# A decoder trunk's feed-forward: its second product by seven products of halves instead of eight

## The chip, the cores and the metric

The kernel runs on one core of a Trainium2 chip. Five engines work side by side, each through its own instructions in order: TensorE (PE, matrix products into PSUM banks), VectorE (DVE, elementwise work), ScalarE (ACT, activation functions and copies), GpSimd (POOL) and SyncE (SP, which here only issues transfers). They wait for each other by semaphores. Transfers between the main memory (HBM) and the on-chip memory (SBUF) are issued by SP, ACT or POOL and carried out by 16 DMA engines. The metric is the device time of one execution in microseconds.

## The reference

A trunk of two layers over 512 tokens of width 1024, in float32. Each layer first mixes the tokens (a gated linear recurrence beside one kind of attention in the first layer, a gated convolutional recurrence beside another kind in the second), projects, adds, normalises; then comes the feed-forward that matters here:

```python
def swiglu(x, w13, w2):
    a, b = jnp.split(x @ w13, 2, axis=-1)
    return (jax.nn.silu(a) * b) @ w2
...
x = layer_norm(ALPHA * x + swiglu(x, ffn_w13[layer], ffn_w2[layer]), ln_g[layer, 1], ln_b[layer, 1])
```

The inner width is 2816, 22 blocks of 128. The first product (gate and up) makes the inner activations, the second (`w2`, 2816 x 1024) brings them back to width 1024. ALPHA is the square root of 2.

## The kernel before, in words

**Three matmuls for one.** PE works in a fast rounded float32 form. To keep the accuracy every operand is split into a rounded high half and a low half (the rest); `mm3` (L252) multiplies high by high, high by low and low by high. A weight tile of 128 x 1024 is loaded by SP into a staging tile `ws` (two of them), ACT copies the high half into `wh`, DVE subtracts for the low half `wl` (`weights`, L231; five buffers each of `wh` and `wl`). A buffer comes free when PE has done the matmuls that read it, and ACT and DVE work in order, so a split that waits for its buffer or its transfer holds up what is queued behind it. Activations are split in the same way by `put` (L247).

**The feed-forward** (`ffn`, L393) takes the 22 inner blocks in parts. For each block of a part, gate and up are made with the inner block on the partitions and the 512 tokens along the free axis: 8 blocks of the width, `mm3` each, into two banks named `pf` (pair `g` for even blocks, pair `s` for odd). ACT applies the SiLU, DVE multiplies by the other bank, `put` splits the result into `hh` and `hl`. When a part's blocks are done, `out_stream` (L375) does its share of the second product: for each half of the 1024 output columns four banks, one for each 128 tokens, gather over the part's blocks, activations held in PE, 512 weight columns moving. Then `add_res` (L327) adds the four banks to the residual `xt` on DVE. The part that comes last goes through `out_rows` (L335), which finishes one token block after the other, since the normalisation follows it. The parts are 6, 6, 6 and 4 blocks in layer 0 and 4, 6, 6 and 6 in layer 1 (`W2_PARTS`, L52).

**The order** of the work on each engine is set by a scheduler that follows the program with priorities; weight splits get a slightly higher one. SP's loads run ahead as far as staging tiles are free. POOL has little to do: constants at the start, some small transfers of 4 KB in the first layer, and one small power (`rs`) for each token block of a normalisation.

## Time and profile before

| | us |
|---|---|
| median of 3 runs | 1257.22 (1256.35 to 1257.58) |
| the profiled execution | 1257.87 |
| its span, first to last instruction | 1256.1 |

| stretch of the span (us) | PE busy | DVE busy | ACT busy | DMA share |
|---|---|---|---|---|
| 297 to 660, feed-forward of layer 0 | 362.81 of 363.00 | 149.35 | 96.63 | 0.32 |
| 890 to 1240, feed-forward of layer 1 | 350.00 of 350.00 | 139.06 | 89.37 | 0.30 |

The granted clock of PE is 0.995 of full speed over the span, and 1.00 in both stretches. Busy means that at least one instruction was at work on the engine. PE's matmuls overlap, so the length of one in the profile is not the time by which it delays the next. "A <- B" in a wait names who waited and who ended the wait. An idle engine that nobody waits for costs nothing.

### The profile page before, as it was taken

To read this page: it belongs to the slowest core of one execution; us is meant where nothing else is said; L and a number is where in the kernel's file an instruction comes from. 1 tells how busy PE (TensorE), PEld (TensorE's weight loads), DVE (VectorE), ACT (ScalarE), POOL (GpSimd) and SP (SyncE) were. 2 spreads that over 40 slices of the span, in tenths; PEclk is the share of its full clock that TensorE was granted. 3 is DMA by queue.
4 is the path that set the end of the run, shared out by engine and by line. 5 is a ranking of instruction groups with operands and counts; after the bars stand their busy time and mean duration, and the time that the engine had idled before them with its cause. 6 is when DMAs were issued, how large, how long until landed. Compare 5 with 4: busy or idle time off the path is not lost.

```text
span 1256.1 us, 15372 instructions
## 1 busy us (share of the span) xinstructions
PE 1233.1 (98%) x6215; PEld 1003.6 (80%) x6215; DVE 689.3 (55%) x1037; ACT 483.2 (38%) x738; POOL 27.1 (2%) x49
## 2 busy tenths in 40 slices
PE   8999999999999999999999998999999999999997
PEld 6787777679888888888888776778988888888886
DVE  6638789668233324334388596687734333324346
ACT  6446567533222222222233757672322222222220
POOL 2000000000000000000000000000000000000001
PEclk9999999999999999999999998999999999999999
DMA  6421211234233233323324231102423333333221
GB/s 239 151 71 56 77 52 51 78 91 151 67 101 89 96 101 101 95 91 101 101 87 131 68 100 34 51 17 84 152 69 100 101 100 90 96 101 101 94 74 67
DMA packets 35271, 115.45 MB, mean 92 GB/s; under 512 B 4208, under 2 KB 5616, under 8 KB 35200
## 3 DMA queue, kind: packets, MB, share of 16 engines
q1 hardware_dynamic: 33648, 112.70, 28.7%
q10 hardware_dynamic: 1296, 1.73, 0.4%
q8 instruction: 49, 0.80, 0.3%
q14 instruction: 22, 0.18, 0.0%
q0 software_dynamic: 256, 0.03, 0.0%
HBM read 112.32 MB, written 2.10 MB: 91 GB/s over the span
## 4 chain that ended last, share of the span: by engine, by line
PE 89%; DVE 6%; ACT 2%; DMA 2%; issue 1%; SPq 0%; DVEq 0%; ACTq 0%
PE pf L255 13%; PE pf L254 13%; PE pf L256 13%; PE po L256 8%; PE po L254 8%; PE po L255 8%; PE pj L255 4%; PE pj L254 4%; PE pj L256 4%; DMA ws<-in_wst 1%; PE sc L528 1%; PE pv L255 1%; PE pv L254 1%; PE pv L256 1%; PE tr L321 1%; PE cu L840 1%
## 5 line engine op out<-in xcount | busy, mean ns | idle before, releaser
L243 ACT CAST wh<-ws 128x1024 fp32r<-128x1024 f32 x175 | 183.9, 1051 | 517.5 <-PE pf L255 182.9
L244 DVE TENSOR_TENSOR wl<-ws,wh 128x1024 fp32r<-128x1024 f32 x175 | 214.2, 1224 | 289.8 <-ACT wh L243 283.8
L255 PE MATMUL pf<-xl,wh 128*128 128x512 f32 x640 | 249.3, 390 | 0.0
L254 PE MATMUL pf<-xh,wh 128*128 128x512 f32 x640 | 249.3, 390 | 0.0
L256 PE MATMUL pf<-xh,wl 128*128 128x512 f32 x640 | 249.3, 390 | 0.0
L256 PEld LDWEIGHTS pf<-xh,wl 128*128 128x128 f32 x640 | 120.2, 188 | 24.9
L255 PEld LDWEIGHTS pf<-xl,wh 128*128 128x128 f32 x640 | 120.2, 188 | 24.9
L254 PEld LDWEIGHTS pf<-xh,wh 128*128 128x128 f32 x640 | 120.2, 188 | 24.7
L254 PE MATMUL po<-wh,hh 128*128 128x512 f32 x336 | 131.2, 390 | 0.0
L256 PE MATMUL po<-wh,hl 128*128 128x512 f32 x336 | 130.9, 390 | 0.2 <-DVE hl L250 0.2
L255 PE MATMUL po<-wl,hh 128*128 128x512 f32 x336 | 130.9, 390 | 0.0
L422 DVE TENSOR_TENSOR s<-s,pf 128x512 f32<-128x512 f32 x44 | 30.3, 688 | 147.3 <-PE pf L256 147.3
L254 PE MATMUL pj<-xh,wh 128*128 128x512 f32 x256 | 104.2, 407 | 2.8 <-DVE qk L617 1.2
L255 PE MATMUL pj<-xl,wh 128*128 128x512 f32 x256 | 103.6, 405 | 0.2 <-DVE xl L250 0.2
L256 PE MATMUL pj<-xh,wl 128*128 128x512 f32 x256 | 103.8, 405 | 0.0
L256 PEld LDWEIGHTS po<-wh,hl 128*128 128x128 f32 x336 | 63.0, 188 | 13.6 <-DVE hl L250 0.6
L254 PEld LDWEIGHTS po<-wh,hh 128*128 128x128 f32 x336 | 63.1, 188 | 13.1 <-ACT hh L249 0.2
L255 PEld LDWEIGHTS po<-wl,hh 128*128 128x128 f32 x336 | 63.1, 188 | 12.9
L254 PEld LDWEIGHTS pj<-xh,wh 128*128 128x128 f32 x256 | 48.5, 189 | 14.3 <-issue 3.0
L256 PEld LDWEIGHTS pj<-xh,wl 128*128 128x128 f32 x256 | 48.4, 189 | 10.1 <-issue 1.6
L255 PEld LDWEIGHTS pj<-xl,wh 128*128 128x128 f32 x256 | 48.4, 189 | 10.0 <-issue 1.1
L332 DVE TENSOR_TENSOR xt<-xt,po 128x512 f32<-128x512 f32 x64 | 43.3, 684 | 22.8 <-PE po L256 22.8
(245 smaller groups left out, 1830.1 us busy)
## 6 DMA issues: line engine op xcount, KB each, us to landing
ws<-in_wst SPq DMA_DIRECT2D x189, 512.0 KB, 3.5
gb<-in_lnp SPq DMA_DIRECT2D x8, 512.0 KB, 5.0
ws<-in_wst SPq DMA_DIRECT2D x11, 256.0 KB, 5.2
xt<-in_xT SPq DMA_DIRECT2D x8, 256.0 KB, 5.6
xt<-in_x SPq DMA_DIRECT2D x1, 2048.0 KB, 8.1
out_y<-xt SPq DMA_DIRECT2D x4, 256.0 KB, 2.0
out_y<-xt ACTq DMA_DIRECT2D x4, 256.0 KB, 2.0
gw<-in_gw ACTq DMA_DIRECT2D x2, 256.0 KB, 2.7
```

The costliest lines, as they stand in the source:

```text
L243: nc.scalar.copy(hi, st)
L244: nc.vector.tensor_tensor(lo, st, hi.bitcast(F32), ALU.subtract)
L254: mm(ps, ah, bh, start=first, stop=False)
L255: mm(ps, ah, bl, start=False, stop=False)
L256: mm(ps, al, bh, start=False, stop=last)
L321: nc.tensor.transpose(ps[:, j * P:(j + 1) * P], y[:, h * T + j * P:h * T + (j + 1) * P], self.ident)
L332: self.nc.vector.tensor_tensor(y, y, ps, ALU.add)
L422: nc.vector.tensor_tensor(s, s, pb, ALU.mult)
L528: nc.tensor.matmul(ps[u:u + 64, g * 256 + c * 64:g * 256 + (c + 1) * 64], E[:, c * P + u:c * P + u + 64], rhs, start=True, stop=True)
L840: nc.tensor.matmul(ps[:, c:c + m], w, x[:, oi:oi + m], start=n == 0 and x is sh, stop=n == len(mms) - 1 and x is sl)
```

## The change

The second product of two parts of 8 inner blocks in each layer is done by a scheme of seven products of halves. The parts become 8, 8, 2 and 4 blocks in layer 0 and 8, 8 and 6 in layer 1. Only the parts of 8 use the new scheme; the others go on as before.

The inner blocks of such a part form four pairs of an even and an odd block. Write u for the even block's activations and v for the odd one's, 0 and 1 for the first and second 256 tokens, and W11, W12, W21, W22 for the weights (first digit: even or odd block, second: first or second half of the output columns). Instead of the eight products of a half with a half there are seven, of these activations ("forms") with these sums:

| product | activations | weights | bank pair | goes to (token half, column half) |
|---|---|---|---|---|
| 1 | u0 | W11 | a | + (1,1), and stays in a |
| 2 | v1-u1 | W11+W12 | c | - (2,2), and stays in c |
| 3 | s2 = u1-u0-v1 | W11+W12+W22 | a, on top | - (1,2) |
| 4 | s4 = u0-u1+v1-v0 | W22 | c, on top | - (1,2) |
| 5 | u0-u1 | W22+W12 | a, on top | - (2,2) |
| 6 | v0 | W21 | d | + (1,1) |
| 7 | v1 | W11+W12+W22+W21 | a, on top | + (2,1) |

The bank pairs hold two blocks of 128 tokens each; a is `sc` and `ho`, c is `pt` and `po`, d the two banks of `s`. What stays in a bank is added to by the next product that uses it, after DVE has read the bank into `xt`.

The weight sums are made by transfers. Two held tiles (x, one for each two pairs of blocks) begin as W11; when ACT and DVE have split a held tile, POOL issues a transfer that adds the next weights from HBM into it, and it is split again. Two more (y) begin as W22 and get W12 added. The tiles take the places `wah` and `wal`, the split halves go through `wh` and `wl` as before. `forms` makes the differences on DVE when a pair of blocks is done and splits each into halves.

```diff
@@ -49,7 +49,9 @@
 BANKS = {"g": 2, "s": 2, "sc": 1, "ho": 1, "pt": 1, "po": 1}
 EARLY = (S_IA, S_IA + 1, S_IA + 2, S_IA + 3)
 
-W2_PARTS = (((0, 6), (6, 12), (12, 18), (18, 22)), ((0, 4), (4, 10), (10, 16), (16, 22)))
+W2_PARTS = (((0, 8), (8, 16), (16, 18), (18, 22)), ((0, 8), (8, 16), (16, 22)))
+H2 = T // 2
 
 
 class Trunk:
@@ -249,11 +251,11 @@
         self.nc.scalar.copy(hi, dst)
         self.nc.vector.tensor_tensor(lo, dst, hi.bitcast(F32), ALU.subtract)
 
-    def mm3(self, ps, ah, al, bh, bl, first, last):
+    def mm3(self, ps, ah, al, bh, bl, first, last, **kw):
         mm = self.nc.tensor.matmul
-        mm(ps, ah, bh, start=first, stop=False)
-        mm(ps, ah, bl, start=False, stop=False)
-        mm(ps, al, bh, start=False, stop=last)
+        mm(ps, ah, bh, start=first, stop=False, **kw)
+        mm(ps, ah, bl, start=False, stop=False, **kw)
+        mm(ps, al, bh, start=False, stop=last, **kw)
 
     def gemm_ws(self, w, ps, c0=0, c1=T):
         hi, lo = w
@@ -324,12 +326,12 @@
             nc.scalar.copy(self.xh[o], pv)
             nc.vector.tensor_tensor(self.xl[o], pv, self.xh[o].bitcast(F32), ALU.subtract)
 
-    def add_res(self, tb, h, ps, first):
+    def add_res(self, tb, h, ps, first, op=ALU.add):
         y = self.xt[:, tb, h * T:(h + 1) * T]
         if first:
-            self.nc.vector.scalar_tensor_tensor(y, y, ALPHA, ps, ALU.mult, ALU.add)
+            self.nc.vector.scalar_tensor_tensor(y, y, ALPHA, ps, ALU.mult, op)
         else:
-            self.nc.vector.tensor_tensor(y, y, ps, ALU.add)
+            self.nc.vector.tensor_tensor(y, y, ps, op)
 
 
     def out_rows(self, acts, base, lnidx=None, nxt=None, fin=False):
@@ -390,12 +392,119 @@
                 self.add_res(tb, h, pss[tb], first)
 
 
+    def fm(self, tag):
+        if tag == "act":
+            return self.sb.tile([P, 2, H2], F32R, tag="act", bufs=16, name=self.nm("fm"))
+        return self.t2k("fm", [P, 2, H2], F32R, "fm")
+    def put2(self, src):
+        hi, lo = self.fm("act"), self.fm("fm")
+        self.put(src, hi, lo)
+        return hi, lo
+    def forms(self, s):
+        nc = self.nc
+        q = s.rearrange("p a (h t) -> p (a h) t", t=H2)
+        uv = self.put2(q[:, 0:4:2, :])
+        d = self.t2k("d", [P, 2, H2], tag="d")
+        nc.vector.tensor_tensor(d, q[:, 0:4:3, :], q[:, 1:2, :].to_broadcast([P, 2, H2]), ALU.subtract)
+        dd = self.put2(d)
+        v1 = self.fm("act")
+        self.put(q[:, 3, :], v1[:, 0, :], v1[:, 1, :])
+        nc.vector.scalar_tensor_tensor(q[:, 1, :], d[:, 0, :], -1.0, q[:, 3, :], ALU.mult, ALU.subtract)
+        nc.vector.scalar_tensor_tensor(q[:, 0, :], q[:, 1, :], -1.0, q[:, 2, :], ALU.mult, ALU.subtract)
+        ee = self.put2(q[:, 0:2, :])
+        at = lambda p, i: (p[0][:, i, :], p[1][:, i, :])
+        return {"u0": at(uv, 0), "v0": at(uv, 1), "u0-u1": at(dd, 0), "v1-u1": at(dd, 1),
+                "s4": at(ee, 0), "s2": at(ee, 1), "v1": (v1[:, 0, :], v1[:, 1, :])}
+    def products7(self, fs, base, first):
+        nc = self.nc
+        n = len(fs)
+        seen = set()
+        def load(dst, j, k, c, add=False):
+            m = base + (k - 1) * n + 2 * c
+            src = self.ins["wst"][m:m + 2, :, (j - 1) * T:j * T].rearrange("m p t -> p m t")
+            dst = dst.rearrange("p (m t) -> p m t", t=T)
+            if add:
+                nc.gpsimd.dma_start(dst, src, accum_op=ALU.add)
+            else:
+                nc.sync.dma_start(dst, src)
+        def split(st):
+            hi, lo = [self.sb.tile([P, D], F32R, tag=t, bufs=5, name=self.nm(t)) for t in ("wh", "wl")]
+            with self.tc.high_priority(offset=self.hp):
+                self.put(st, hi, lo)
+            return hi, lo
+        def held(tag, j):
+            ts = [self.t2k("w" + tag, [P, D], tag=tag) for _ in range(n // 2)]
+            for c, t in enumerate(ts):
+                load(t, j, j, c)
+            return ts
+        def plain(j, k):
+            ws = []
+            for c in range(n // 2):
+                st = self.sb.tile([P, D], F32, tag="ws", bufs=2, name=self.nm("ws"))
+                load(st, j, k, c)
+                ws.append(split(st))
+            return ws
+        def summed(ts, nxt=None):
+            ws = []
+            for c, t in enumerate(ts):
+                ws.append(split(t))
+                if nxt:
+                    load(t, *nxt, c, True)
+            return ws
+        def product(ws, name, ps, start=False, stop=False):
+            for m, f in enumerate(fs):
+                (hi, lo), (ah, al) = ws[m // 2], f[name]
+                c = slice(m % 2 * T, m % 2 * T + T)
+                for b in range(2):
+                    t = slice(b * P, (b + 1) * P)
+                    self.mm3(ps[b], ah[:, t], al[:, t], hi[:, c], lo[:, c], start and m == 0, stop and m == n - 1,
+                             skip_group_check=True)
+        def result(i, k, ps, op):
+            for b in range(2):
+                self.add_res(2 * (i - 1) + b, k - 1, ps[b], first and (i, k) not in seen, op)
+            seen.add((i, k))
+        a = [self.bank(t, "fa") for t in ("sc", "ho")]
+        c = [self.bank(t, "fc") for t in ("pt", "po")]
+        x, y = held("wah", 1), held("wal", 2)
+        product(summed(x, (1, 2)), "u0", a, True)
+        result(1, 1, a, ALU.add)
+        product(summed(x, (2, 2)), "v1-u1", c, True)
+        result(2, 2, c, ALU.subtract)
+        product(summed(x, (2, 1)), "s2", a)
+        result(1, 2, a, ALU.subtract)
+        product(summed(y, (1, 2)), "s4", c, stop=True)
+        result(1, 2, c, ALU.subtract)
+        product(summed(y), "u0-u1", a)
+        result(2, 2, a, ALU.subtract)
+        d = [self.bank("s", "fd") for _ in range(2)]
+        product(plain(2, 1), "v0", d, True, True)
+        result(1, 1, d, ALU.add)
+        product(summed(x), "v1", a, stop=True)
+        result(2, 1, a, ALU.add)
     def ffn(self, base, wa, lnidx, nxt=None):
         nc = self.nc
         idx = base
         parts = W2_PARTS[nxt is None]
         for pi, (k0, k1) in enumerate(parts):
-            acts = []
+            seven = k1 - k0 == 8
+            acts, fs = [], []
             blocks = list(range(k0, k1))
             if pi == 0:
                 groups = [[0, 1]] + [[k] for k in range(2, k1)]
@@ -415,17 +524,23 @@
                 else:
                     for w, ps in zip(ws, pss):
                         self.gemm_ws(w, ps)
-                for i in range(len(g)):
+                for i, k in enumerate(g):
                     pa, pb = pss[2 * i], pss[2 * i + 1]
-                    s = self.t2k("s", tag="s")
-                    nc.scalar.activation(s, pa, AF.Silu)
-                    nc.vector.tensor_tensor(s, s, pb, ALU.mult)
-                    hh, hl = self.act("hh"), self.act("hl")
-                    self.put(s, hh, hl)
-                    acts.append((hh, hl))
-            last = pi == len(parts) - 1
-            if last:
+                    if k % 2 == 0:
+                        s = self.t2k("s", [P, 2, T], tag="s")
+                    h = s[:, k % 2, :]
+                    nc.scalar.activation(h, pa, AF.Silu)
+                    nc.vector.tensor_tensor(h, h, pb, ALU.mult)
+                    if not seven:
+                        hh, hl = self.act("hh"), self.act("hl")
+                        self.put(h, hh, hl)
+                        acts.append((hh, hl))
+                    elif k % 2:
+                        fs.append(self.forms(s))
+            if pi == len(parts) - 1:
                 wa = self.out_rows(acts, idx, lnidx, nxt, nxt is None)
+            elif seven:
+                self.products7(fs, idx, pi == 0)
             else:
                 self.out_stream(acts, idx, pi == 0)
             idx += k1 - k0
@@ -881,13 +996,13 @@
     with t.phase("l0", v=8, p=2, pT=1, E=5, bb=1, kq=1, G=1, acc=1, ks=1, es=1) as t.ph, \
             tc.tile_pool(name="odd", bufs=1) as t.odd:
         y = t.layer0()
-    with t.phase("f0", s=3, wah=4, wal=4) as t.ph:
+    with t.phase("f0", s=2, d=1, fm=12, wah=4, wal=4) as t.ph:
         wa = t.out_rows(y, S_WO0 + 4, 0, S_FFN0)
         wa = t.ffn(S_FFN0, wa, 1, S_XR)
         xr = t.proj_halves(wa)
     with t.phase("l1", v=4, qk=7, kz=2, z=6, l=4, sh=5, sl=5) as t.ph:
         y = t.layer1(xr)
-    with t.phase("f1", s=3, wah=4, wal=4) as t.ph:
+    with t.phase("f1", s=2, d=1, fm=12, wah=4, wal=4) as t.ph:
         wa = t.out_rows(y, S_WO1 + 4, 2, S_FFN1)
         t.ffn(S_FFN1, wa, 3)
```

Three places show how the instructions move. First POOL: in layer 0, behind the powers of the first normalisation (`rs`). Before, the next powers follow at once:

```order
L310 TENSOR_TENSOR rs_2690<-ve_2688,nhalf 128x1 [waits DVE_49,Activation_49]
L310 TENSOR_TENSOR rs_2745<-ve_2743,nhalf 128x1 [waits DVE_49,Activation_49]
L310 TENSOR_TENSOR rs_5017<-ve_5015,nhalf 128x1 [waits DVE_49,Pool_49]
L310 TENSOR_TENSOR rs_5072<-ve_5070,nhalf 128x1 [waits DVE_49,Pool_49]
L310 TENSOR_TENSOR rs_5139<-ve_5137,nhalf 128x1 [waits DVE_49,Pool_49]
```

After the change there are the adding transfers (`wwah` are the held tiles x, `wwal` the tiles y; the eight of the first part, and the first of the second):

```order
L312 TENSOR_TENSOR rs_2745<-ve_2743,nhalf 128x1 [waits DVE_49,Activation_49]
L436 DMA wwah_3433<-in_wst 128x2x512 [waits DMASW7_49,DMASW6_49,DMAHW5_49,DVE_49,Pool_49]
L436 DMA wwah_3434<-in_wst 128x2x512 [waits DMAHW6_49,DVE_49]
L436 DMA wwah_3433<-in_wst 128x2x512 [waits DMASW0_49,DVE_49]
L436 DMA wwah_3434<-in_wst 128x2x512 [waits DMASW1_49,DVE_49]
L436 DMA wwah_3433<-in_wst 128x2x512 [waits DMASW2_49,DVE_49]
L436 DMA wwah_3434<-in_wst 128x2x512 [waits DMASW3_49,DVE_49]
L436 DMA wwal_3437<-in_wst 128x2x512 [waits DMAHW7_49,DVE_49,Activation_49]
L436 DMA wwal_3438<-in_wst 128x2x512 [waits DMAHW0_49,DVE_49]
L436 DMA wwah_4289<-in_wst 128x2x512 [waits DMAHW1_49,DVE_49]
```

Each waits for DVE, which splits the tile; the two adds into y stand behind the third pair of adds into x.

Second ACT, at the end of layer 0's first part, where gate and up end and the second product begins. Before (`s` is the SiLU, `hh` the high half of a block's activations):

```order
L249 CAST hh_3178<-s_3175 128x512 [waits DVE_49]
L243 CAST wh_3355<-ws_3353 128x1024 [waits DMAHW1_49,PE_49,Activation_49]
L421 ACTIVATE s_3244<-pf_3188 128x512 [waits PE_49,Activation_49]
L243 CAST wh_3385<-ws_3383 128x1024 [waits DMAHW2_49,PE_49,Activation_49]
L249 CAST hh_3247<-s_3244 128x512 [waits DVE_49]
L243 CAST wh_3415<-ws_3413 128x1024 [waits DMAHW3_49,PE_49,Activation_49]
L243 CAST wh_3449<-ws_3447 128x1024 [waits DMAHW4_49,PE_49,Activation_49]
L243 CAST wh_3456<-ws_3454 128x1024 [waits DMAHW5_49,PE_49,Activation_49]
```

After (`fm` are the high halves of the forms of the last pair of blocks, in the order u0 and v0, the two differences, v1, then s4 and s2):

```order
L532 ACTIVATE s_3343<-pf_3287 128x512 [waits PE_49,Activation_49]
L251 CAST wh_3477<-wwah_3433 128x1024 [waits DMASW0_49,PE_49,Activation_49]
L251 CAST wh_3482<-wwah_3434 128x1024 [waits DMASW1_49,PE_49,Activation_49]
L532 ACTIVATE s_3343<-pf_3352 128x512 [waits PE_49]
L251 CAST wh_3513<-wwah_3433 128x1024 [waits DMASW2_49,PE_49,Activation_49]
L251 CAST fm_3410<-s_3343 128x512 [waits DVE_49]
L251 CAST fm_3416<-d_3414 128x512 [waits DVE_49]
L251 CAST fm_3420<-s_3343 128x256
L251 CAST wh_3518<-wwah_3434 128x1024 [waits DMASW3_49,PE_49,Activation_49]
L251 CAST wh_3549<-wwal_3437 128x1024 [waits PE_49,Activation_49]
L251 CAST fm_3425<-s_3343 128x512 [waits DVE_49]
L251 CAST wh_3554<-wwal_3438 128x1024 [waits PE_49,Activation_49]
```

The splits for the third product (`wh_3513`, `wh_3518`), which wait for the second adds into x, now stand around the last pair's forms.

Third DVE, in the first part's second product. Before, splits and the adds of four banks `po` alternate:

```order
L244 TENSOR_TENSOR wl_3450<-ws_3447,wh_3449 128x1024 [waits DMAHW4_49,Activation_49]
L330 SCALAR_TENSOR_TENSOR xt<-xt,po_3251 128x512 [waits PE_49]
L330 SCALAR_TENSOR_TENSOR xt<-xt,po_3252 128x512 [waits PE_49]
L330 SCALAR_TENSOR_TENSOR xt<-xt,po_3253 128x512 [waits PE_49]
L330 SCALAR_TENSOR_TENSOR xt<-xt,po_3254 128x512 [waits PE_49]
L244 TENSOR_TENSOR wl_3457<-ws_3454,wh_3456 128x1024 [waits DMAHW5_49,Activation_49]
L244 TENSOR_TENSOR wl_3519<-ws_3516,wh_3518 128x1024 [waits DMAHW6_49,Activation_49]
L244 TENSOR_TENSOR wl_3526<-ws_3523,wh_3525 128x1024 [waits DMAHW7_49,Activation_49]
L330 SCALAR_TENSOR_TENSOR xt<-xt,po_3349 128x512 [waits PE_49]
L330 SCALAR_TENSOR_TENSOR xt<-xt,po_3350 128x512 [waits PE_49]
L330 SCALAR_TENSOR_TENSOR xt<-xt,po_3351 128x512 [waits PE_49]
```

After (`fa` and `fc` are the banks a and c, `wwal` the tiles y):

```order
L418 SCALAR_TENSOR_TENSOR s_3343<-s_3343 128x256 [waits DVE_49]
L332 SCALAR_TENSOR_TENSOR xt<-xt,fa_3429 128x512 [waits PE_49]
L332 SCALAR_TENSOR_TENSOR xt<-xt,fa_3430 128x512 [waits PE_49]
L252 TENSOR_TENSOR fm_3426<-s_3343,fm_3425 128x512 [waits Activation_49]
L252 TENSOR_TENSOR wl_3550<-wwal_3437,wh_3549 128x1024
L252 TENSOR_TENSOR wl_3555<-wwal_3438,wh_3554 128x1024 [waits Activation_49]
L332 SCALAR_TENSOR_TENSOR xt<-xt,fc_3431 128x512 [waits PE_49]
L332 SCALAR_TENSOR_TENSOR xt<-xt,fc_3432 128x512 [waits PE_49]
L252 TENSOR_TENSOR wl_3586<-wwal_3437,wh_3585 128x1024 [waits DMASW6_49,Activation_49]
L252 TENSOR_TENSOR wl_3590<-wwal_3438,wh_3589 128x1024 [waits DMASW7_49,Activation_49]
L332 SCALAR_TENSOR_TENSOR xt<-xt,fa_3429 128x512 [waits PE_49]
L332 SCALAR_TENSOR_TENSOR xt<-xt,fa_3430 128x512 [waits PE_49]
```

The results of the third product (the last two rows) stand behind the two splits of the tiles y that wait for POOL's adds (`DMASW`).

## The prediction

> **What bounds the kernel now.** I read the page's busy shares first, then the waits and the windows of the feed-forward alone, then the starts of single matmuls. TensorE (PE) is busy for 98% of the span. The window row of the first feed-forward (columns: busy and instructions of PE, weight loads, VectorE = DVE, ScalarE = ACT, GpSimd = POOL; granted clock, DMA share, GB/s) shows it without a gap, at clock 1.00. Behind it stand its only wait there, and two groups of waits of ACT.
>
> ```profile
> PE 1233.1 (98%) x6215; PEld 1003.6 (80%) x6215; DVE 689.3 (55%) x1037; ACT 483.2 (38%) x738; POOL 27.1 (2%) x49
> ...
> 300.00:620.00 320.00, 320.00 (x1481) 268.08 (x1480) 117.02 (x130) 83.96 (x101) 0.92 (x1) 1.00 0.32 99
> ...
> PE po L256 <- DVE hl L250: 0.2, 1, 0.2
> ...
> ACT wh L243 <- PE pf L255: 93.4, 24, 4.2
> ACT wh L243 <- PE po L256: 64.7, 15, 4.4
> ```
>
> ACT waits for PE (weight buffers come free as PE finishes with them), PE waits for nobody. So here a matmul less is time less, as long as what feeds PE keeps up. What a matmul is worth must be read from starts, not from its mean. The rows give minimum, median and maximum duration, then first and last start: the first stream of the second product (L254, 48 of its 144 matmuls), the next gate-and-up stretch (288 in all), and the two matmuls at the border between them.
>
> ```profile
> L254 PE MATMUL po<-wh,hh x48: 388/390/390, 360.4 to 392.3; 128*128 128x512 f32 x48
> ...
> L254 PE MATMUL pf<-xh,wh x96: 388/390/390, 393.0 to 457.6; 128*128 128x512 f32 x96
> ...
> 392.79 0.39 PE L256 MATMUL po<-wh,hl 128*128 128x512 f32 x1
> 393.01 0.39 PE L254 MATMUL pf<-xh,wh 128*128 128x512 f32 x1
> ```
>
> Each lasts 0.39 us, yet the next starts 0.22 us later: they overlap. From 360.4 to 393.0 stand 144 starts, 0.2264 us each. I use 0.2267, which the 288 up to 458.29 (quoted below) give.
>
> **The matmuls.** A product of halves is 4 block pairs x 2 token blocks x 3 = 24 matmuls; seven are 168, where 8 blocks x 4 x 2 x 3 = 192 stood. That is 24 fewer in each of four parts, 96 in all; the order of the instructions agrees (5597 rows on PE become 5501). 96 x 0.2267 = **21.8 us**. The form of the matmul is the old one: activations held, 512 weight columns moving.
>
> That the duration misleads is also said by the Trainium skill (Perfetto Trace Analysis, Identifying the Most-Contended Engine): PE's busy share is no measure, because matmuls are pipelined. Priced by the duration the gain would be 96 x 0.39 = 37.4 us; by the starts it is 21.8, and the trace agrees with the rule.
>
> **What is added off PE.** A part has 14 weight splits where 8 blocks had 8, seven results of two adds where a stream had 8 adds, and the forms. Durations:
>
> ```profile
> L244 DVE TENSOR_TENSOR wl<-ws,wh 128x1024 fp32r<-128x1024 f32 x58 | 71.1, 1225 | 124.9 <-ACT wh L243 122.3
> L422 DVE TENSOR_TENSOR s<-s,pf 128x512 f32<-128x512 f32 x20 | 13.7, 687 | 68.7 <-PE pf L256 68.7
> L250 DVE TENSOR_TENSOR hl<-s,hh 128x512 fp32r<-128x512 f32 x20 | 13.7, 685 | 1.4 <-ACT hh L249 1.4
> L330 DVE SCALAR_TENSOR_TENSOR xt<-xt,po 128x512 f32<-128x512 f32 x8 | 5.5, 688 | 2.1 <-PE po L256 2.1
> ...
> L243 ACT CAST wh<-ws 128x1024 fp32r<-128x1024 f32 x57 | 60.1, 1054 | 226.1 <-PE pf L255 93.4 <-PE po L256 64.7 <-issue 50.7
> L249 ACT CAST hh<-s 128x512 fp32r<-128x512 f32 x20 | 12.4, 621 | 5.5 <-DVE s L422 5.5
> ```
>
> The seven products last 168 x 0.2267 = 38.1 us. In that time DVE has about 14 splits (17.2), 14 adds (9.6) and the last pair's forms (five ops of 512 and three of 256 columns; the latter between half of 0.69 and all of it, I take 0.36: 4.5), 31 us of 38. ACT has some 18. Both fit, so as sums they cost nothing, under PE's matmuls; without that cover DVE's 31 would stand beside 38. What matters is order. Three places, counted from the first matmul of the first product (t = 0, each product 5.44 long).
>
> *Border from gate-and-up to products.* The same border stands in the trace (PE, DVE, ACT):
>
> ```profile
> 458.29 0.39 PE L254 MATMUL po<-wh,hh 128*128 128x512 f32 x1
> ...
> 458.56 0.69 DVE L422 TENSOR_TENSOR s<-s,pf 128x512 f32<-128x512 f32 x1 [3.38 <-PE pf L256]
> 459.39 1.23 DVE L244 TENSOR_TENSOR wl<-ws,wh 128x1024 fp32r<-128x1024 f32 x1
> 460.54 0.69 DVE L250 TENSOR_TENSOR hl<-s,hh 128x512 fp32r<-128x512 f32 x1
> ...
> 458.31 1.05 ACT L243 CAST wh<-ws 128x1024 fp32r<-128x1024 f32 x1 [3.90 <-issue]
> 459.28 0.62 ACT L249 CAST hh<-s 128x512 fp32r<-128x512 f32 x1
> ```
>
> The gate's product begins at 0.27. Now DVE does the differences d (0.69), a split (1.23) and the low half of the last pair's u0 and v0 (0.69) behind it: 0.27 + 0.69 + 0.69 + 1.23 + 0.69 = 3.6. The first product needs it at its 21st matmul, 20 x 0.2267 = 4.5. Cover 0.9 us, cost 0; every us beyond it costs 4 in all. In layer 0's new short stream (blocks 16 and 17) the low half, 2.94 us after the border in these rows, is needed at the 15th matmul, 3.2: 0.
>
> *The adds.* No add of a transfer into a tile is in this trace; its price has to be bounded. The rows: a plain load of 512 KB, two at once, one of 2048 KB, and POOL's small transfers with their time on the engine; then the bytes and the share of the 16 engines that they took in 320 us.
>
> ```profile
> ws<-in_wst SPq DMA_DIRECT2D x58, 512.0 KB, 3.5
> gb<-in_lnp SPq DMA_DIRECT2D x2, 512.0 KB, 4.9
> ...
> xt<-in_x SPq DMA_DIRECT2D x1, 2048.0 KB, 8.1
> ...
> k<-c POOLq DMA_DIRECT2D x8, 4.0 KB, 1.6
> ...
> 155.60 0.52 POOL L632 DMA_DIRECT2D k<-c  x1 [46.49 <-PE s L655]
> ...
> q1 hardware_dynamic: 8614, 31.35, 31.8%
> ```
>
> 31.35 MB took 31.8% of 320 us, 101.8 us of all engines: 1.7 us for 512 KB. The other 1.8 of the 3.5 are fixed; 2.0 with POOL's slower issue. An add must read the tile as well as the weights. Its transfer time q is at least 1.7 (as cheap as a load); with two reads for one it is 3.4; with three passes 5.1. I take **3.4**, since a second read is what the operation has to do and nothing shows a third. No row shows POOL making the pieces of so large a transfer; 5.1 stands for that too, and more is not excluded.
>
> *The tight place* is the fourth and fifth product, which both come from the second pair of held tiles. DVE's order behind the 3.6 above: low half of the differences (4.3), of v1 (4.6), a form (5.0), a split (6.2), a form (6.6), two results (7.9), a low half (8.6), the two splits of the fourth product (9.8 and 11.0). Only then may POOL start their adds, and ahead on its queue stand the third adds into the first pair (issued at about 2.9 and 6.2). With q = 3.4 the four move one behind another: 4.9 to 8.3, to 11.7, 11.8 to 15.2, to 18.6. Then ACT (1.05) and DVE (1.23) split, and DVE, which works in order, has the third product's first result (0.69) queued behind that split: 21.6. PE wants that bank back at 4 x 5.44 = 21.8. **Cost 0, with 0.2 us to spare.** From there the stall in each part is 4.9 + 4q + 3.0 - 21.8 = 4q - 13.9. At 1.7 there is none; at 5.1 it is 6.5, four times 26 us. The earlier adds have 6 us or more (5.4 wanted), the two later products 3 us of slack or more. POOL's other work, the powers of the normalisation, comes a part later.
>
> *Transfers.* SP issues all eight held loads of a layer in one row as soon as block pair 0 and 1 is done; the weight behind them (block 5's second) is not used by PE before 7 x 5.44 = 38 us later, eight loads take 8 x 1.7 = 13.6: 0. The two plain loads of the sixth product use the old staging.
>
> **Sum.** The profiled execution took 1257.87 us (span 1256.1): 1257.87 - 21.8 + 0 = 1236.1. It lay 0.65 above the median of the runs shown, 1257.22, so on the median's scale **1235.5 us**.
>
> **Rivals.**
>
> *Partly late adds.* q between 3.5 and 4.8. For it: the second read goes into SBUF that loads do not read, and its 2 KB pieces are half the loads' 4 KB. Against it: 4.9 us for two loads in flight is 1.4 more than one, so an engine queues no worse than by size. At q = 4.2: stall 2.9 a part, 11.6: 1247.1 us.
>
> *Slower: the adds bind.* From q = 4.84 the stall of 5.44 a part eats the whole gain. The one mechanism is DVE's order: the third product's results stand behind a split that waits for the fourth tile's add, and PE waits for the results. At 5.1: 1235.5 + 26 = 1261.5 us. For it: an unseen operation, on a queue that here moved 4 KB at a time. Against: nothing in the rows costs three passes.
>
> *POOL starved by DVE.* If POOL could write its transfer's pieces only while DVE pauses, the adds of the fourth product would start at 12.5, when DVE's run with the second product's results ends: 14.5 + 2 x 3.4 = 21.3, stall 2.5 a part, 10: 1245.5 us. The Trainium skill warns of such a lock (SBUF — State Buffer, Who interferes with whom), for DVE's copies and not for its two-input operations. POOL's row above lasted its 0.52 us while DVE worked, as did the others like it, which speaks against it.
>
> *The duration counts.* 96 x 0.39: 1219.8 us. The starts exclude it as far as I can see.
>
> **How the numbers follow.** Forecast 0.53, partly late 0.19, adds bind 0.18, POOL starved 0.07, duration 0.03. The measurement tells 0.2% (2.5 us) from no change. Faster: the forecast, nearly all of the partly late, the last two: 0.79; within 0.2%: the strip of q around 4.84, 0.04; slower 0.17. Low end: 1235.5 less 3.5, for the spread of 1.2 us between runs and PE's 1256.1 - 1233.1 = 23 us of idle time elsewhere that may shift. High end: q = 4.5, 4 x 4.1 above the forecast, 1252. The likeliest case alone: 1234 to 1238.
>
> **What would show it.** In the window of a part's products PE is busy without a gap, 24 starts to 5.44 us. Adds land within 5.5 us alone and 8 in a row. If I am wrong in the tight place, PE waits there for DVE's result into xt behind a split, and the split's ACT half for a POOL transfer; landing then exceeds 9 us. If the border fails, PE waits at the 19th to 21st matmul of the first product for an activation's low half. If DVE's load is what fails, waits of PE for weight halves appear with the adds long landed.

## The result, and the profile after

The changed kernel takes 1235.03 us (median of 4 runs, 1234.23 to 1238.23) where before took 1257.4. The ratio is 0.983, its 95% interval 0.981 to 0.985. The profiled execution took 1234.23 us (span 1232.5), 23.6 less than the profiled one of before.

First the busy shares of the page after and the window row of the first feed-forward (columns as in the prediction's first fence), then the moments of POOL's power `rs`, which stands at the end of each normalisation: the first and the fifth, which enclose layer 0's feed-forward, and the ninth and thirteenth, which enclose layer 1's.

```profile
PE 1211.2 (98%) x6119; PEld 984.2 (80%) x6119; DVE 760.5 (62%) x1157; ACT 522.3 (42%) x794; POOL 66.1 (5%) x81
...
300.00:620.00 320.00, 320.00 (x1476) 267.63 (x1475) 158.91 (x197) 107.49 (x134) 20.28 (x17) 1.00 0.47 122
...
274.33 0.94 POOL L312 TENSOR_TENSOR rs<-ve,nhalf 128x1 f32<-128x1 f32 x1 [71.54 <-DVE ve L310]
628.78 0.93 POOL L312 TENSOR_TENSOR rs<-ve,nhalf 128x1 f32<-128x1 f32 x1 [110.37 <-DVE ve L310]
856.53 0.92 POOL L312 TENSOR_TENSOR rs<-ve,nhalf 128x1 f32<-128x1 f32 x1 [184.68 <-DVE ve L310]
1202.34 0.93 POOL L312 TENSOR_TENSOR rs<-ve,nhalf 128x1 f32<-128x1 f32 x1 [101.40 <-DVE ve L310]
```

The same four of before:

```profile
275.38 0.94 POOL L310 TENSOR_TENSOR rs<-ve,nhalf 128x1 f32<-128x1 f32 x1 [71.47 <-DVE ve L308]
640.51 0.92 POOL L310 TENSOR_TENSOR rs<-ve,nhalf 128x1 f32<-128x1 f32 x1 [338.33 <-DVE ve L308]
869.67 0.92 POOL L310 TENSOR_TENSOR rs<-ve,nhalf 128x1 f32<-128x1 f32 x1 [185.60 <-DVE ve L308]
1226.17 0.92 POOL L310 TENSOR_TENSOR rs<-ve,nhalf 128x1 f32<-128x1 f32 x1 [329.72 <-DVE ve L308]
```

PE still has no gap in the window, with 96 matmuls fewer on the page (6215, now 6119). Layer 0's feed-forward went from 365.13 to 354.45 us, layer 1's from 356.50 to 345.81: 10.7 each, 21.4 together. The other 2.2 us of the profiled difference lie outside (1.05 before the first mark and 1.4 in the second layer's mixing, less 0.2 behind the last mark). The stretch before the first mark lasts 272.6 to 276.8 us over all kernels of this study, so its part is scatter. The mixing lasts 229.2 to 229.8 us in the three kernels whose first layer has the old stream and 227.1 to 228.7 in the eleven others.

More than half of the mixing's 1.4 us goes with the clock. PE waits there 2.4 us for DVE (bank `cu`), in every kernel of this study, and behind that wait its granted clock drops to one half, for 6.8 us in before's profile and for 3.4 in the changed kernel's. The windows of the 8 us from that place on, before's and then after's, have a clock of 0.57 and 0.79 (the third column from the right):

```profile
768.00:776.00 8.00, 7.19 (x30) 6.22 (x30) 6.08 (x11) 3.58 (x6) 0.00 (x0) 0.57 0.08 32
...
756.00:764.00 8.00, 7.20 (x35) 5.63 (x36) 6.28 (x10) 3.15 (x6) 0.00 (x0) 0.79 0.03 12
```

Among the eleven, the mixing took 228.4 to 228.7 us in the six profiles with 6.8 us of half clock and 227.1 to 228.3 in the five with 3.4. The three all have 6.8 and lie 0.4 to 1.4 us above those six; that may belong to the change and was not followed up.

Now the tight place, in layer 0's first part. The first product begins at 381.1, which is the prediction's t = 0. POOL's rows of the last four adds, ACT's and DVE's rows of the two splits that wait for y's adds with the results behind them, and PE at the border to the fifth product:

```profile
384.18 1.20 POOL L436 DMA_DIRECT2D wwah<-in_wst  x1 [4.72 <-DMA wwah<-in_wst]
387.19 1.20 POOL L436 DMA_DIRECT2D wwah<-in_wst  x1 [1.81 <-DVE wl L252]
390.72 1.20 POOL L436 DMA_DIRECT2D wwal<-in_wst  x1 [2.33 <-ACT wh L251]
392.08 1.20 POOL L436 DMA_DIRECT2D wwal<-in_wst  x1 [0.16 <-issue]
...
397.03 1.05 ACT L251 CAST wh<-wwal 128x1024 fp32r<-128x1024 f32 x1 [6.51 <-DMA wwal<-in_wst]
399.57 1.05 ACT L251 CAST wh<-wwal 128x1024 fp32r<-128x1024 f32 x1 [1.50 <-DMA wwal<-in_wst]
...
400.66 1.22 DVE L252 TENSOR_TENSOR wl<-wwal,wh 128x1024 fp32r<-128x1024 f32 x1 [1.32 <-ACT wh L251]
401.80 1.28 DVE L332 SCALAR_TENSOR_TENSOR xt<-xt,fa 128x512 f32<-128x512 f32 x2
...
402.82 0.39 PE L256 MATMUL fa<-wh,fm 128*128 128x512 f32 x1
```

y's adds are issued at t = 9.7 and 11.0 (predicted 9.8 and 11.0). The first is split at 16.0, where the prediction had it land at 15.2; the second is split at 18.5 (predicted landing 18.6). The first result behind that split is done at 401.80 + 0.68 = 402.48, and PE takes the bank at 402.82 without having waited: 0.3 us to spare, where the prediction had 0.2. In the same profile the spare time of the other three parts, read in the same way, is 0.3, 0.6 and, in layer 1's second part, nothing.

What an add costs stands in the row of POOL's queue (packets, MB, share of the 16 engines) in the stretch from 290 to 660 us, and in the page's rows from issue to landing:

```profile
q0 software_dynamic: 4352, 8.39, 14.4%
...
wwah<-in_wst POOLq DMA_DIRECT2D x24, 512.0 KB, 5.9
wwal<-in_wst POOLq DMA_DIRECT2D x8, 512.0 KB, 6.7
```

16 adds took 14.4% of 370 us: q = 3.33 us each. The prediction had 3.4.

### The profile page after: what moved, and what is told of

Same layout as the page of the kernel before. It is cut to its first block, busy times and chain, and to the rows that moved or that the text cites. A ratio compares the mean times of both kernels' runs of the same rounds, so it can differ in the third digit from the quotient of the medians.

```text
span 1232.5 us, 15454 instructions
## 1 busy us (share of the span) xinstructions
PE 1211.2 (98%) x6119; PEld 984.2 (80%) x6119; DVE 760.5 (62%) x1157; ACT 522.3 (42%) x794; POOL 66.1 (5%) x81
## 4 chain that ended last, share of the span: by engine, by line
PE 90%; DVE 6%; ACT 2%; DMA 1%; issue 1%; SPq 0%; DVEq 0%; ACTq 0%
PE pf L257 13%; PE pf L256 13%; PE pf L258 13%; PE pj L257 5%; PE pj L256 5%; PE pj L258 5%; PE po L258 4%; PE po L256 4%; PE po L257 4%; PE fa L256 2%; PE fa L258 2%; PE fa L257 2%; PE sc L643 1%; PE fc L258 1%; PE fc L257 1%; PE fc L256 1%
## 5 line engine op out<-in xcount | busy, mean ns | idle before, releaser
L245 ACT CAST wh<-ws 128x1024 fp32r<-128x1024 f32 x143 | 150.2, 1051 | 309.1 <-PE pf L257 119.1
L246 DVE TENSOR_TENSOR wl<-ws,wh 128x1024 fp32r<-128x1024 f32 x143 | 174.9, 1223 | 155.2 <-ACT wh L245 150.4
L251 ACT CAST wh<-wwah 128x1024 fp32r<-128x1024 f32 x32 | 33.7, 1054 | 74.9 <-PE pf L257 63.3
L256 PE MATMUL po<-wh,yh 128*128 128x512 f32 x128 | 51.4, 402 | 0.0
L258 PE MATMUL po<-wh,yl 128*128 128x512 f32 x128 | 51.1, 399 | 0.0
L257 PE MATMUL po<-wl,yh 128*128 128x512 f32 x128 | 50.8, 397 | 0.0
L252 DVE TENSOR_TENSOR wl<-wwah,wh 128x1024 fp32r<-128x1024 f32 x32 | 38.7, 1220 | 18.5 <-ACT wh L251 17.9
L256 PE MATMUL fa<-wh,fm 128*128 128x512 f32 x128 | 49.9, 390 | 0.0
L257 PE MATMUL fa<-wl,fm 128*128 128x512 f32 x128 | 49.8, 389 | 0.0
```

What stands on the lines that cost most here:

```text
L245: nc.scalar.copy(hi, st)
L246: nc.vector.tensor_tensor(lo, st, hi.bitcast(F32), ALU.subtract)
L251: self.nc.scalar.copy(hi, dst)
L252: self.nc.vector.tensor_tensor(lo, dst, hi.bitcast(F32), ALU.subtract)
L256: mm(ps, ah, bh, start=first, stop=False, **kw)
L257: mm(ps, ah, bl, start=False, stop=False, **kw)
```

## Experiments

The kernels were run in three groups on three chips. Before, measured again beside each group, took 1256.5 to 1257.3 us; the ratios are to that. In the diffs `...` stands for lines left out.

### The cuts without the seven products

```diff
-            seven = k1 - k0 == 8
+            seven = False
```

> The changed kernel with its new part cuts (8, 8, 2, 4 blocks and 8, 8, 6), but every part's second product by the old stream of eight products. Theory (all of the gain is the 96 matmuls that the seven products leave out): 96 matmuls more than the changed kernel, as many as before the change, so the time of before, 1257 us, within 2 us. Rival (the longer parts gave some of the gain, by fewer borders between gate-and-up and second product): below 1254 us, and the part below 1257 is what the cuts gave.

1256.89 us, ratio to before 1.000 (0.999 to 1.001). The new cuts gave nothing; all of the gain belongs to the seven products.

### The seven products in one layer

```diff
-            seven = k1 - k0 == 8
+            seven = k1 - k0 == 8 and nxt is None
```

> Seven products only in the two parts of the second layer; the first layer has the new cuts and the old stream. Theory (each part of seven products is worth 24 x 0.2267 = 5.44 us, wherever it stands): two parts, 10.9 us, so 1257.4 - 10.9 = 1246.5 us, within 1.5. Rival (the two layers' gains differ, since a layer's feed-forward starts from another place in the program and its third part is another): over 1.5 us away from it.

1248.33 us, ratio 0.993 (0.991 to 0.995), so 9.0 us faster (6.8 to 11.2), where 10.9 was expected. The median lies 1.8 above the expected 1246.5, over the 1.5 that I gave the theory, though the interval holds 10.9. The waits of PE in layer 1 (us in total, times, longest) show where part of it went, which the changed kernel's profile did not have:

```profile
PE fa L256 <- ACT wh L251: 1.1, 2, 0.7
```

Layer 1's feed-forward took 347.14 us in this profile, 9.4 less than before's and 1.3 more than the changed kernel's. So the tight place, the same program text, costs something in some executions. That led to the last experiments.

### Plain transfers in place of the adds

```diff
-                nc.gpsimd.dma_start(dst, src, accum_op=ALU.add)
+                nc.gpsimd.dma_start(dst, src)
```

> The 32 adding transfers become plain transfers of the same size on the same queue: the weight sums are left out (a held tile is overwritten by the next weights). Theory (the adds move in 3.3 us each and are hidden): no gain, the time of the changed kernel, 1235 us within 1.5; POOL's queue falls from 8.6% of the span to about half of it, since an add moves its bytes twice. Rival (late adds cost something in some of the four parts): 1.5 us or more below the changed kernel.

This kernel leaves the weight sums out. It takes 1234.83 us (1233.63 to 1236.34), as the changed kernel: the adds are hidden, to within the microsecond or two that the tight place costs in some executions. The queue's row for the same stretch, the landing, and POOL's own time for these transfers (sum, mean in ns):

```profile
q0 software_dynamic: 2304, 8.39, 7.8%
...
wwah<-in_wst POOLq DMA_DIRECT2D x12, 512.0 KB, 3.9
...
L436 POOL DMA_DIRECT2D wwah<-in_wst x24 | 17.5, 728 | 396.6 <-DVE wl L252 396.6
```

7.8% of 370 us are 1.80 us a transfer: for the same bytes an add takes 1.85 times a load's transfer time and nearly twice its packets, and lands some 2 us later. The prediction's middle value, 3.4, was the right one, and 5.1 was not. That the second read is what costs is not shown by itself: the add's packets are also half as large (8.39 MB in 4352 packets against 2304).

### Extras behind every add

```diff
                 nc.gpsimd.dma_start(dst, src, accum_op=ALU.add)
+                real = self.newest()
+                nc.gpsimd.dma_start(more, src[:, 0, 0:496], accum_op=ALU.add)
+                self.behind(self.newest(), real)
...
-        product(summed(y), "u0-u1", a)
+        ws = summed(y)
+        for r in third:
+            self.behind(r, self.newest())
+        product(ws, "u0-u1", a)
```

`behind(a, b)` fixes that a stands behind b on its engine; `third` holds the third product's two results.

> Behind each adding transfer a further adding transfer of 128 x 496 (248 KB, not quite half an add) goes into a tile that nobody reads, on the same queue; the order on DVE in the tight place stays (results of the third product behind the two splits of the tiles y). Theory (the chain of the prediction: adds move one behind another, the second add into y is split, the third product's results are queued behind that split, and PE waits for the bank): three such extras, 1.6 us each, lie ahead of the landing of y's second add, 4.7 to 4.9 us, less the 0.35 us that the changed kernel's trace shows to spare: about 4.4 us a part, 17 in all, 1252 us (1248 to 1256), and PE waits for DVE's results (xt from the banks fa) at the first matmul of the fifth product and nowhere else. Rival (the adds have more room than that, or extras move beside the adds): 1237 us or less.

1266.69 us (1265.1 to 1270.63), slower than before: ratio 1.007 (1.005 to 1.009), and 14.7 us over the theory. PE's waits in the whole program, POOL's rows around y's adds, PE behind the first wait, and a window two microseconds long behind it:

```profile
PE fa L256 <- ACT wh L251: 25.0, 4, 6.9
...
393.75 0.90 POOL L439 DMA_DIRECT2D more<-in_wst  x1 [5.06 <-DMA more<-in_wst]
394.31 1.57 POOL L437 DMA_DIRECT2D wwal<-in_wst  x1
...
409.88 0.77 PE L256 MATMUL fa<-wh,fm 128*128 128x512 f32 x1 [6.60 <-ACT wh L251]
410.44 0.63 PE L257 MATMUL fa<-wl,fm 128*128 128x512 f32 x1
...
411.00:413.00 2.00, 2.00 (x6) 1.52 (x5) 1.95 (x4) 0.00 (x0) 0.00 (x0) 0.50 0.23 31
```

The place is the one foretold, four times and nowhere else. Two things make it dearer. The first is my edit: all extras go into one tile, so each waits on POOL for the one before to land (5.06 us in the second row here), and y's adds are issued late beyond what the extras move. The second is PE: after the wait its matmuls last 0.63 us and start 0.43 apart, at a granted clock of 0.50 in the window's row, and return to 0.39 and 0.23 at 414.7. The feed-forwards lost 34.9 us to the changed kernel's (rows of `rs` as above), of which 25.0 are waits; four slow restarts of ten matmuls at 0.2 us each are 8.

### One extra between y's adds

```diff
...
                 if nxt:
                     load(t, *nxt, c, True)
+                    if ts is y and c == 0:
+                        real = self.newest()
+                        nc.gpsimd.dma_start(more, self.ins["wst"][base + 8][:, 0:496], accum_op=ALU.add)
+                        self.behind(self.newest(), real)
...
```

The rest of the edit makes the extra's tile, fills it with zeros in each part, and fixes DVE's order in the tight place as in the changed kernel.

> Only one extra adding transfer of 128 x 496 in a part, between the add into the first tile y and that into the second; everything else as in the changed kernel, DVE's order in the tight place too. Theory (the spare time there is the 0.35 us that the trace shows; every us beyond it costs PE a us): 1.6 - 0.35 = 1.2 us a part, 5 in all: 1240 us (1238 to 1242). Rival (there is more spare time, the adds do not wait for each other): 1235 us, as the changed kernel.

1240.31 us (1239.81 to 1241.29), ratio 0.987 (0.985 to 0.989): as the theory had it. ACT's split of y's second tile comes 4.68 us behind the first, where the changed kernel had 2.54, and PE waits:

```profile
397.82 1.05 ACT L251 CAST wh<-wwal 128x1024 fp32r<-128x1024 f32 x1 [6.24 <-DMA wwal<-in_wst]
402.50 1.05 ACT L251 CAST wh<-wwal 128x1024 fp32r<-128x1024 f32 x1 [3.63 <-DMA wwal<-in_wst]
...
404.72 1.28 DVE L332 SCALAR_TENSOR_TENSOR xt<-xt,fa 128x512 f32<-128x512 f32 x2
...
405.55 0.47 PE L256 MATMUL fa<-wh,fm 128*128 128x512 f32 x1 [1.51 <-ACT wh L251]
```

The profile names ACT's split as releaser, but that ended at 403.55; the first result, begun at 404.72, was done at 405.40, 0.15 before PE. (A wait for several semaphores is put down to one of them.) The four waits are 1.51, 0.55, 0.71 and 0.86; none is followed by matmuls of 0.63 us. A filling of the extra's tile stands on DVE ahead of y's splits here and waits for the extra, to 400.01; but DVE then waited for ACT's split of the second tile all the same, so the filling does not set the time.

### Extras behind every add, results ahead of the splits

The edit on POOL is that of the kernel with extras behind every add; on DVE `split` of the tiles y is put behind the two results:

```diff
-        def split(st):
+        def split(st, after=()):
...
+            for r in after:
+                self.behind(self.newest(), r)
...
-        product(summed(y), "u0-u1", a)
+        product(summed(y, after=third), "u0-u1", a)
```

> The extras behind every add as in the kernel that doubles half of each add, but on DVE the third product's two results are placed ahead of the two splits of the tiles y. Theory (it is DVE's order that turns a late add into a wait of PE: the bank comes free only behind the split): PE then waits only for the second tile's weights, of which the fifth product needs the second tile from its 13th matmul on, 2.7 us later than the bank; most of the stall goes, 0 to 0.9 us a part remain: 1235 to 1239 us. Rival (the late weights themselves hold PE, whatever the order): as with the extras alone, about 1252 us.

1259.48 us (1255.92 to 1262.83): neither. One row of DVE says why the time tells nothing:

```profile
406.62 0.47 DVE L493 MEMSET more<- 128x496 f32 x1 [10.78 <-DMA more<-in_wst]
```

This is my own filling of the next part's extra tile with zeros. In the first part of each layer it stood between the first and the second result and held DVE, for 10.78 us in this row, until the last extra had landed; PE waited 7.4 and 6.7 us there. The second parts have no such filling, and there the trace does answer. PE in layer 0's second part:

```profile
539.85 0.51 PE L256 MATMUL fa<-wh,fm 128*128 128x512 f32 x1 [1.08 <-ACT wh L251]
541.11 0.50 PE L257 MATMUL fa<-wl,fm 128*128 128x512 f32 x1 [0.75 <-DVE wl L252]
```

In both second parts PE waits only for the second tile's weights, 1.8 us here and 2.2 in layer 1, where the kernel with extras behind every add waited 5.4 and 6.1. That is the theory's direction, though more than its 0 to 0.9 us. The question was put again without the filling (below).

### y's adds ahead of x's third adds

```diff
...
-        product(summed(x, (2, 1)), "s2", a)
+        ws = summed(x)
+        product(ws, "s2", a)
         result(1, 2, a, ALU.subtract)
-        product(summed(y, (1, 2)), "s4", c, stop=True)
+        ws = summed(y, (1, 2))
+        last = self.newest()
+        for i, t in enumerate(x):
+            load(t, 2, 1, i, True, last)
+        product(ws, "s4", c, stop=True)
```

`last` is the second add into y; the lines left out let `load` put a transfer behind it.

> No extras. POOL issues the third adds into the tiles x behind the adds into the tiles y instead of ahead of them, so that y's adds land some 6 us earlier. Theory (in the changed kernel the adds land just in time and cost nothing): median as the changed kernel, 1235 us within 1; the seventh product, which needs the third adds, has 3 us or more left. Rival (adds that land late in some executions make the spread of the changed kernel, 1234.2 to 1238.2 us): faster by 0.5 us or more, and its runs within 1 us of each other.

1237.17 us (1236.56 to 1241.43), ratio 0.985 (0.983 to 0.987): not faster, and as far apart from run to run as the changed kernel. Both expectations were wrong about the adds, since y's do not land earlier:

```profile
390.64 1.20 POOL L436 DMA_DIRECT2D wwal<-in_wst  x1 [11.26 <-ACT wh L251]
392.73 2.95 POOL L436 DMA_DIRECT2D wwah<-in_wst  x2
...
400.25 1.05 ACT L251 CAST wh<-wwal 128x1024 fp32r<-128x1024 f32 x1 [2.45 <-PE fc L258]
```

They are issued at the same moments as in the changed kernel, when DVE has split the tiles; by the prediction's own sum (11.7 against 11.8) x's third adds were just out of the way by then. The second is split 0.7 us later than there. (The row names PE as releaser; in the other three parts the split waits for the transfer, and it stands at t = 19.1 to 19.9, where the changed kernel's first profile has 18.3 to 18.8.) So PE waits in all four parts, 0.40, 0.50, 1.00 and 0.25 us. That the transfers now right behind it share the engines with it would explain this, but was not shown.

### DVE copies while POOL issues

```diff
...
                     load(t, *nxt, c, True)
+                    real = self.newest()
+                    for _ in range(4 * (ts is x and nxt == (1, 2))):
+                        nc.vector.tensor_copy(more, self.xh[:, 0, 0:496].bitcast(F32))
+                        self.behind(self.newest(), real)
```

> Behind each of the first adds into the tiles x DVE makes four copies of 128 x 496 (float32, SBUF to SBUF, into a tile that nobody reads), which run while POOL issues that add. It tests the rule of the Trainium skill (SBUF - State Buffer, Who interferes with whom) by which DVE's copies hold POOL off from writing a transfer's pieces. Theory (no such hold here): POOL's rows for these adds last their 1.20 us as in the changed kernel, and the time stays at 1235 us within 2. Rival (the rule): these rows last longer, by up to the 4 copies' time; DVE has room, so the time would still be under 1240 us.

1236.37 us (1235.79 to 1236.8), ratio 0.984 (0.982 to 0.985). The second add of the part and the copies over it:

```profile
368.16 1.21 POOL L436 DMA_DIRECT2D wwah<-in_wst  x1 [4.25 <-DVE wl L252]
...
367.77 1.85 DVE L468 COPY more<-xh 128x496 f32<-128x496 f32 x4
```

Four copies run from 367.77 to 369.62, over the whole of POOL's row, which lasts the usual 1.21 us; the median landing of the adds into x stays at 5.9 us. The Trainium skill (SBUF — State Buffer, Who interferes with whom) has copies that can hold off POOL's writing of a transfer's pieces; no row here shows it. (This profile has the tight place's waits too, 0.37 and 0.96 us in layer 1.)

### One extra ahead of both y adds

```diff
-                    if ts is y and c == 0:
+                    if ts is x and c == 1 and nxt == (2, 1):
```

against the kernel with one extra between y's adds; its tile is filled once a layer.

> One extra adding transfer of 128 x 496 in a part, as in the kernel with one extra between the two adds into the tiles y, but ahead of both: behind the third add into the second tile x, which is POOL's last transfer before y's. DVE's order in the tight place as in the changed kernel. Theory (the prediction's chain: the third adds into x, moving one behind another, end at 11.7, just when y's first add could start at 11.8): the extra of 1.6 us moves y's adds by 1.5 us, less the 0.35 to spare: 1.1 us a part, 4.6 in all, 1239.6 us (1238 to 1241). Rival (x's adds end well before y's are issued, so an extra there fits into a gap): 1235 us, within 1.5.

1243.79 us (1241.27 to 1245.63), ratio 0.989 (0.988 to 0.991); the changed kernel in the same rounds took 1236.16. The rival falls: x's third add, the extra and y's adds do move one behind another. But 7.6 us is more than 4.6. The extra moves y's second split further than the 1.5 us of the theory, in the first part from t = 18.5 to 20.8. PE's four waits are 1.88, 1.24, 1.95 and 0.91, 6.0 us, and two of them have a sequel. PE's rows at the first, and the window of the 5 us around it:

```profile
406.96 0.47 PE L256 MATMUL fa<-wh,fm 128*128 128x512 f32 x1 [1.88 <-ACT wh L251]
...
408.00 0.63 PE L257 MATMUL fa<-wl,fm 128*128 128x512 f32 x1
...
406.00:411.00 5.00, 4.04 (x12) 3.18 (x13) 5.00 (x8) 1.80 (x2) 0.00 (x0) 0.69 0.20 66
```

After the waits of 1.88 and 1.95 us, and not after those of 1.24 and 0.91, about eight matmuls run at half the clock, beginning a microsecond after PE has started again: 8 x 0.2 = 1.6 us each. The profiled execution is the slowest of the four (1245.63 us).

### One extra between y's adds, results ahead of the splits

```diff
                     load(t, *nxt, c, True)
+                    if ts is y and c == 0:
...
-        product(summed(y), "u0-u1", a)
+        product(summed(y, after=third), "u0-u1", a)
```

The extra is that of the kernel with one between y's adds; its tile is filled once a layer.

> One extra adding transfer of 128 x 496 between the two adds into the tiles y, as before (that cost 5.3 us), but DVE has the third product's two results ahead of the two splits of the tiles y that wait for the adds. Its own tile is filled with zeros once a layer, ahead of the parts, so that nothing on DVE waits for the extra (in the kernel with extras behind every add such a fill stood ahead of the results and held them until the extra had landed). Theory (DVE's order alone makes the wait): y's second tile is split at 24.2 at the latest where the fifth product's 13th matmul wants it at 24.5: 1235 us within 1.5. Rival (the late weights hold PE by themselves): 1240 us, as with the old order.

1234.06 us (1232.7 to 1235.37), ratio 0.982 (0.980 to 0.983). The 5.3 us that the same extra cost (1240.31 against 1235.03; 4.6 in the feed-forwards of the two profiles) are gone, and PE's waits with them. The adds were late: DVE begins the split of y's second tile at t = 20.6 to 20.9 in the four parts, where the kernel with the old order has 20.5 to 21.5 and waits. So it is DVE's order that makes a late add a wait of PE; the weights themselves have time.

### That order alone, and the changed kernel beside it

```diff
-        product(summed(y), "u0-u1", a)
+        product(summed(y, after=third), "u0-u1", a)
```

> No extras: the changed kernel with only DVE's order altered, the third product's results ahead of the two splits of the tiles y. Theory (the tight place costs nothing in some executions and up to 1 us in a part in others, as the traces of some of the other experiments show): the wait goes in all of them; 0.5 to 2 us faster than the changed kernel in the same round, and runs closer together. Rival (the spread of the changed kernel comes from outside the feed-forward): no difference over 0.5 us.

> The changed kernel itself, unaltered, on the same chip and in the same rounds as the three others, so that differences of a microsecond can be read. Both theories: 1235 us, within 1.5; if the tight place makes part of its spread, PE shows in its trace waits of 0.3 to 1 us for the split of y's second tile where it is slow and none where it is fast.

1234.4 us (1232.98 to 1236.07), ratio 0.982 (0.981 to 0.983), against 1236.16 us (1234.53 to 1238.89), ratio 0.984 (0.982 to 0.985). The medians differ by 1.8 us, within the 0.5 to 2 expected, but the runs overlap and so do the intervals: the times alone don't settle it. The traces say more. The changed kernel's second profile, of an execution of 1238.89 us (the issue of y's second add, its split, DVE's results behind it, and PE), then the new order's (DVE's first result at once behind PE's product, the second split behind it, that split in layer 1's second part, and the window of layer 0):

```profile
393.24 1.20 POOL L436 DMA_DIRECT2D wwal<-in_wst  x1 [0.16 <-issue]
...
402.13 1.05 ACT L251 CAST wh<-wwal 128x1024 fp32r<-128x1024 f32 x1 [2.90 <-DMA wwal<-in_wst]
...
404.36 1.28 DVE L332 SCALAR_TENSOR_TENSOR xt<-xt,fa 128x512 f32<-128x512 f32 x2
...
405.18 0.47 PE L256 MATMUL fa<-wh,fm 128*128 128x512 f32 x1 [1.05 <-ACT wh L251]
```

```profile
397.77 1.37 DVE L332 SCALAR_TENSOR_TENSOR xt<-xt,fa 128x512 f32<-128x512 f32 x2 [3.92 <-PE fa L258]
...
401.90 1.23 DVE L252 TENSOR_TENSOR wl<-wwal,wh 128x1024 fp32r<-128x1024 f32 x1 [1.63 <-ACT wh L251]
...
1110.75 1.23 DVE L252 TENSOR_TENSOR wl<-wwal,wh 128x1024 fp32r<-128x1024 f32 x1 [2.36 <-ACT wh L251]
...
300.00:620.00 320.00, 320.00 (x1480) 267.80 (x1479) 160.25 (x199) 107.53 (x134) 20.28 (x17) 1.00 0.46 121
```

In that second profile PE waits 1.05, 0.59 and 0.35 us in three of the four parts, and its two feed-forwards are 1.4 us longer each than in the changed kernel's first profile. With the new order PE waits for nothing in the four parts. In the first part shown that is no proof, since the split of y's second tile (401.90, t = 20.0) is hardly later than in the changed kernel's first profile (19.6). But in layer 1's second part it begins at t = 20.8, where the old order made PE wait: 0.86 us at 20.8 with one extra between y's adds, 1.05 at 21.0 in the second profile above.

What was late in that second profile is the end of the add only. In the two microseconds ahead of ACT's split the mean busy share of the 16 DMA engines is 0.10 (the second column from the right), so at most a few were still at work. In the first profile the share is 0.99 until half a microsecond before that split.

```profile
400.20:402.20 2.00, 2.00 (x11) 1.65 (x10) 0.29 (x1) 0.07 (x1) 0.00 (x0) 1.00 0.10 18
```

Why a few engines finish late is not shown.

## Why the prediction was right

**The matmuls.** 96 fewer, 21.8 us by starts; the feed-forwards lost 21.4. The cuts alone gave 0. The price by the start (0.2267) stands, that by the duration (37.4) is out.

**Off PE.** The window of the first part's products after, and DVE's low half of the last pair:

```profile
382.00:421.00 39.00, 39.00 (x174) 32.30 (x173) 28.34 (x36) 15.83 (x19) 4.81 (x4) 1.00 0.62 132
...
383.79 0.68 DVE L252 TENSOR_TENSOR fm<-s,fm 128x512 fp32r<-128x512 f32 x1
```

DVE was busy for 28.3 of 39 us (predicted 31 of 38), PE for all 39. The border held: the low half ended at t = 3.4 (predicted 3.6).

**The adds.** q is 3.33 where 3.4 was taken from the bounds 1.7 and 5.1. "Adds land within 5.5 us alone" was short by half a microsecond: 5.9 on the median (5.8 the shortest), 2.6 of it beside the transfer time, where I had 2.0.

**The tight place.** Issue and last landing hold within 0.2 us in the first part of the first profile; between them the first of y's adds is split 0.8 us later than the chain has it landing, with the second 2.5 us behind it and not 3.4, so the two move partly together. The mechanism, the third product's results behind a split that waits for an add, was shown from both sides: an extra costs some 5 us with that order and nothing with the other. "Cost 0, with 0.2 us to spare" is right for the first profile only, and there one part of four has nothing to spare. From issue to split y's second add took 7.5 us there and 8.9 in the second, and this scatter is larger than the spare time; the cost is then up to 1 us in a part.

**The rivals.** "Slower: the adds bind" named the right mechanism, and with enough on the queue it happens: the kernel with extras behind every add is slower than before, at the place named. Its price 4q - 13.9 was too low for the longer waits, since PE restarts at half the clock after them, and since the shared tile of the extras issues y's adds late. "POOL starved" got no support from the copies. Partly late adds is what some executions show, at no more than a quarter of the 11.6 us that I gave it: 2.8 in the second profile.

**The span.** 2.2 us of the profiled difference are not from the feed-forward and were not forecast; 1.05 of it is scatter before the first mark, and some 0.8 goes with how long PE's clock stayed low behind the same wait. The cost of the waits in the tight place, up to 2.8 us in a run, was not forecast either and pulls the other way. That the median of 1235.03 came within half a microsecond of 1235.5 is luck to that extent; the 21.4 us of the feed-forwards are not.

## What to carry to other kernels

Where PE is busy throughout, price a matmul less by the distance of starts, and spend the effort on the order of the engine that frees PE's banks. On an engine that works in order, put what releases a bank ahead of what waits for a transfer: that order here costs nothing that the times show and takes away the dependence on when a transfer lands. An experiment's own additions (a shared target tile, a fill) bring waits too; read the trace of the experiment before its time.

## What the runs showed of the hardware

- An adding transfer of 512 KB, float32, from HBM into SBUF took 3.33 us of all 16 DMA engines where a plain one on the same queue took 1.80, had 4352 packets for 2304 in 16 transfers, and held POOL for 1.21 us against 0.73.
- PE's wait has a price beyond its length. Every one costs some 0.2 us more: the matmuls on either side no longer overlap (0.39 - 0.23 = 0.16) and the first lasts 0.47 where others last 0.39. With one extra between y's adds the feed-forwards lost 4.6 us for 3.6 us of waits, four of them.
- Behind a longer wait PE runs at half the clock. In the tight place nothing of the kind followed single waits of 1.51 us and less; after 1.88, 1.95 and more, eight to ten matmuls ran 0.43 us apart. Two waits close together did it too, once of two: 1.48 and 0.76 us were followed by half the clock, 1.08 and 0.75 were not (extras behind every add, results ahead). The low clock lasted 3.4 or 6.8 us each time. The length of the wait alone does not decide: in the first layer's mixing a wait of 1.8 us at the same instruction (bank `s`) was followed by 6.8 us of half clock in five of the 14 profiles, by 3.4 in eight and by none in one, and the stretch before the first mark lasted 275.4 to 276.8, 274.1 to 275.4 and 272.6 us in that order. That is much of the scatter outside the feed-forwards. The Trainium skill (TensorE: Matmul & The Clock Gate, The HAM clock gate) has PE fall to half its clock after an idle window of about 3.4 us, and such a gate fits what is seen; but here a wait of 1.9 us was enough, twice out of two in the tight place.
- The same program's add, issued at t = 11.0 in both, was there for its split at t = 18.5 in one execution and at 19.9 in another. A margin of 0.3 us is none.
